# The first half's input projection reads x channel by channel: two products on raw x, token roots applied behind them, no transposes of x

## The chip, the cores and the metric

The kernel runs on one core of a Trainium2 chip. The metric is the device time of one execution in microseconds (us). The kernel before takes 2466.52 us (median of three runs, 2465.56 to 2467.81). In the profile, PE is the matrix engine (TensorE), PEld its weight loads, DVE the vector engine, ACT the scalar engine, POOL the GpSimd engine, SP the engine whose queue issues most DMAs.

## What is computed

One layer of an encoder on x, 2048 tokens of 1024 channels, in float32. Only its first step matters here: a root-mean-square norm of each token, then one wide projection.

```python
def rmsnorm(x, g):
    y = x * rsqrt(mean(x * x, axis=-1, keepdims=True) + 1e-6) * g
    return y

xn = rmsnorm(x, norm1_g[l])          # (2048, 1024)
z = xn @ w_in[l]                     # 1024 x 4608
u_pool, zq, zf, zi, zo, zg = split(z, [512, 1024, 1536, 2048, 2560])
q = silu(zq); f = lb + (1 - lb) * sigmoid(zf); v = zi
o = hgrn2(q, f, v) * silu(zo)        # gated linear recurrence
...                                  # pooling branch, gates, merge, FFN, final norm
```

The factor `rsqrt(...)` is one number for each token; it is called the token's root below.

## The kernel before

The 2048 tokens are worked through in two passes of 1024 (`b0` = 0 and 2 of the loop at the end). A pass runs `mixer` (projections, recurrence, pooling branch, output product) and `ffn`. Inside a pass, the two blocks of 512 tokens are the row halves of a Strassen-Winograd scheme: instead of eight block products each projection takes seven, P1 to P7, on sums and differences of the blocks of x (`B11`, `B21`, `B22`, `T1` to `T4`, table `FORM`) and of the weights. B11 and B21 are the low and high 512 channels of the first token block, B12 and B22 those of the second; T2 is B11 plus or minus blocks of the second token block, and so on. Each operand is split into a rounded high part and a rest (`split`: the high part by an ACT cast, the rest by a DVE subtraction), and a product is three matmuls: high by high, high by low, low by high.

The first projection of a pass, `proj_io`, computes zi and zo. It has 28 steps: seven products (order `IO_ORDER`: P1, P2, P6, P5, P7, P4, P3) times four blocks of 128 channels, each step 12 matmuls of 128x512 into four PSUM banks named `io_X`, `io_Y`, `io_Z`, `io_V` (`n_step`). In the traces its matmuls carry those names; the projections after it are called `fr_`, `gr_`, `ur_`. The weights come through `Stream`: SP loads a raw tile of 256 KB, `convert` makes the pair of parts (tile `ops`: ACT cast, DVE subtraction), at most six pairs ahead. The weights of P6 are sums of three raw tiles, made in `plan_io` (tiles `w8s` to `w11s`, line 406), on DVE.

In the first pass, the operand side works like this. `load_x_tile` loads x in rows (token on the partition). ACT squares with an accumulator give each token's sum of squares, POOL makes the root (`row_rstd`), DVE multiplies the rows by it (line 743, `x_xs`). PE transposes 128x128 pieces (line 829, `x_t`), so that channels lie on the partitions; ACT and DVE read the transposed tiles from PSUM, apply the gain and make the two parts (`scaled`, lines 868 and 869). The second token block is treated the same way a little later by `forms_b_task`. PE runs 44 more transposes of `ident` that nobody reads (`warm`): 24 ahead of the first x and five behind each of the first four row tiles. The masks of the recurrence are made on POOL by `setup_task` (lines 643 to 672), started ahead of P7 and let run when the task is stepped. The Tile scheduler decides where the instructions of these tasks stand on each engine; hand-set ties (`behind`, `stream.pins`) hold some of them.

In the second pass (`b0` = 2) the same projection already takes x channel by channel (`channel_forms`).

Of the kernel before, what the change touches and what calls it, by code (L numbers as in the profile page):

```python
# [18 lines left out]
P = 128  # L19
# [45 lines left out]
GO_AT = 3  # L65
LEAD = 5
X_AT = 8
WARM = 24, 5
GO_IO = (("P2", 1), ("P2", 0))
G_POOL = 4  # L70
CW_AT = 2
# [9 lines left out]
N_OPS = 6  # L81
LOOKAHEAD = 4
MM_PER_TICK = 6


@with_exitstack
def tile_trunk(
# [28 lines left out]
    def slot(name, cols=TB, dt=F32):  # L116
        return slots.tile([P, cols], dt, tag="s", name=name, padded_shape=[P, 528])
# [248 lines left out]
    def plan_one(key, src):  # L366
        r = stream.raw(src)
        stream.op(key, lambda nm, r=r: r.tile, [r])

    SUM_OF = {"P5": "s1", "P6": "s2", "P7": "s3", "P3": "s4"}  # L370

    def plan_io(b0):
        sevens = {}
        for p in IO_ORDER:
            for k in range(4):

                q = [w_io[k, :, c * 512 : (c + 1) * 512] for c in (0, 3, 1, 2)]
                one = {"P1": 0, "P2": 1, "P4": 3}
                if p in one:
                    plan_one("io", q[one[p]])  # L380
                    continue
                if b0:
# [16 lines left out]
                def fn(nm, k=k, p=p, raws=raws):  # L399
                    if p != "P6":  # L400
                        keep(("io", k, p), raws[0].tile, True)
                        return raws[0].tile
                    t = raws[0].tile
                    for i, r in enumerate(raws[1:]):
                        t2 = slot(f"{nm}s{i}")
                        dve.tensor_tensor(t2, t, r.tile, ALU.add)
# [195 lines left out]
    cols = const.tile([P, at], F32, tag="cols", name="cols")  # L602
    act.dma_start(cols, params)

    for j in range(1, NT):
        load_x_tile(0, j)
    for _ in range(N_RAW):
        stream.load()

    def col(o):  # L610
        return cols[:, o : o + 1]

# [2 lines left out]

    neghalf = const.tile([P, 4], F32, tag="neghalf", name="neghalf")
    pool.memset(neghalf, -0.5)

    lbt = const.tile([P, 4, 4], F32, tag="lbt", name="lbt")

# [87 lines left out]
    def warm(n, other=None):  # L708
        ps = bank("warm", P)
        for _ in range(n):  # L710
            ins = pe.transpose(ps, ident, ident)
            if other is not None:
                behind(ins, other)

    last_root = [None]

# [16 lines left out]
    def norm_rows(src, name, xs, after, lag=1):  # L733
        for j in range(NT):
# [8 lines left out]
                dve.tensor_scalar(t[hf], halves[hf], r[:, 0:1], None, ALU.mult)  # L743
                xs[j, hf] = t[hf]
            after(j)

    def load_channels(b, k):
        t = slot(f"xc{b}_{k}")
        sp.dma_start(t, x_ct[k * P : (k + 1) * P, b * TB : (b + 1) * TB])
        return t  # L750

    def root_rows(b, name):
        ss = small.tile([P, 2, 4], F32, tag="ssx", name=f"{name}ss")
# [273 lines left out]
        return forms, first, Task(channels_b_task(b + 1, gain, forms, full, go))  # L1027

    def need(forms, key, late):
        task = forms["task"][0] if key in ("B11", "B21") else late  # L1030
        while len(forms[key]) < 4:
            task.step()
        return forms[key]


# [376 lines left out]
    def proj_io(b0, forms, late, vd, zd):  # L1412
# [40 lines left out]
        for p in IO_ORDER:  # L1453
# [6 lines left out]
            for k in range(4):  # L1460
# [30 lines left out]
                        after(p, j)  # L1491
                stream.used(1)

    def mixer(b0, forms, late):
# [5 lines left out]
        proj_io(b0, forms, late, vd, zd)  # L1500
        if b0 == 0:
# [518 lines left out]
        return nxt[0] if nxt else None  # L2020


    nxt = forms_of("x", 0, o_n1, early=True, go=lambda: go_io[0])
    for _ in range(5):
        nxt[1].step()
    load_rows(1)
    while len(nxt[0]["B11"]) < 4:
        nxt[1].step()
# [5 lines left out]
    dve.tensor_tensor(lbt[:, 2], lbt[:, 0], lbt[:, 0], ALU.subtract)  # L2034
    dve.tensor_scalar(lbt[:, 3], lbt[:, 2], -1.0, 1.0, ALU.mult, ALU.add)
    for b in range(0, SEQ // TB, 2):
        forms, task, late = nxt
        if b:
            join(task)
        forms, task, late = mixer(b, forms, late)  # L2040
        join(task)
        nxt = ffn(b, forms, late)
# [51 lines left out]
```

## Time and profile before

| | us |
|---|---|
| median of 3 runs | 2466.52 |
| the profiled execution's own time | 2465.07 |
| its span in the trace | 2463.4 |
| DVE busy in it | 1921.5 |
| ACT busy in it | 1229.6 |
| POOL busy in it | 776.4 |

The span is what the trace covers; the time has 1.7 us around it. Busy times are sums of the recorded durations. A row of the timeline gives start and duration in us, engine, line, operation, output and inputs by name, shape and count; in brackets stands the idle time ahead of it and what ended it. A duration runs from the moment an instruction's semaphores are met to its end, so a wait inside the engine is part of it. Two rows that follow each other may overlap by some 0.08 us.

### The profile page before, as it was taken

What the parts mean: (1) busy time and instruction counts of PE and PEld (TensorE: products, weight loads), DVE (VectorE), ACT (ScalarE), POOL (GpSimd) and SP (SyncE); (2) the same over time, 40 slices, a digit from 0 to 9 for tenths busy, and PEclk for the clock granted to TensorE, in tenths of its full rate; (3) what the DMA queues carried; (4) which work ended last, traced back from release to release, by engine and by line L of the source; (5) the groups of instructions that cost most, each with busy time, mean ns of one, the idle gap of its engine ahead of it and who ended that gap; (6) DMA issues with size and microseconds to landing.
All of it is one profiled execution on the core that took longest, in us unless ns stands there. A gap on an engine that the chain in (4) does not pass through costs nothing.

```text
span 2463.4 us, 37815 instructions
## 1 busy us (share of the span) xinstructions
PE 2441.2 (99%) x12624; PEld 1977.9 (80%) x12624; DVE 1921.5 (78%) x3310; ACT 1229.6 (50%) x2368; POOL 776.4 (32%) x1080
## 2 busy tenths in 40 slices
PE   9999999999999999999999999999999999999998
PEld 7887777788888888888878888887888888888887
DVE  7777776897998778885596667779889987778755
ACT  6545544435555454553545455542465554445534
POOL 5343353403444333551320101122033332335310
PEclk9999999999999999999999999999999999999999
DMA  8889887777898789897554343456333444447852
GB/s 273 273 221 270 246 220 234 242 231 252 204 262 235 224 226 243 268 361 241 171 193 158 132 131 121 155 201 229 129 130 125 151 156 133 146 146 257 307 167 98
DMA packets 260226, 502.53 MB, mean 204 GB/s; under 512 B 27264, under 2 KB 47872, under 8 KB 259712
## 3 DMA queue, kind: packets, MB, share of 16 engines
q1 hardware_dynamic: 192176, 321.73, 39.8%
q0 software_dynamic: 42880, 113.27, 18.0%
q10 hardware_dynamic: 24976, 65.13, 7.6%
q8 instruction: 99, 1.62, 0.3%
q14 instruction: 95, 0.78, 0.1%
HBM read 388.35 MB, written 189.27 MB: 234 GB/s over the span
## 4 chain that ended last, share of the span: by engine, by line
PE 75%; DVE 5%; issue 1%; DMA 1%; ACT 1%; POOL 1%; SPq 0%; ACTq 0%; DVEq 0%; POOLq 0%
PE dn_P L155 16%; PE up_Z L155 15%; PE up_X L155 10%; PE up_V L155 10%; PE wo_P L155 5%; PE pb L155 3%; PE gr_X L155 2%; PE gr_V L155 2%; DVE ops L252 1%; PE io_Z L155 1%; PE fr_X L155 1%; PE io_V L155 1%; PE fr_V L155 1%; PE gr_Z L155 1%; PE gr_Y L155 1%
## 5 line engine op out<-in xcount | busy, mean ns | idle before, releaser
L251 ACT CAST ops<-raw 128x512 fp32r<-128x512 f32 x792 | 487.3, 620 | 765.5 <-PE dn_P L155 168.2
L252 DVE TENSOR_TENSOR ops<-raw,ops 128x512 fp32r<-128x512 f32 x792 | 589.6, 749 | 235.5 <-ACT ops L251 224.7
L1827 DVE SCALAR_TENSOR_TENSOR e<-h,cols,e 128x512 f32<-128x512 f32 x176 | 143.0, 817 | 30.6 <-ACT e L1825 23.0
L1825 ACT ACTIVATE e<-h,cols 128x512 f32<-128x512 f32 x176 | 142.2, 814 | 25.3 <-DVE h L1275 18.9
L1084 POOL DMA_DIRECT2D g_P<-dg_P x154 | 84.4, 549 | 172.0 <-PE dn_P L155 127.3
L1830 DVE SCALAR_TENSOR_TENSOR e<-h,cols,e 128x512 f32<-128x512 f32 x176 | 133.9, 770 | 2.5
L1396 POOL TENSOR_TENSOR gf_P<-e,e 128x512 f32<-128x512 f32 x44 | 61.0, 1389 | 148.9 <-DVE e L1836 85.9
L473 POOL TENSOR_TENSOR raw<-raw,raw 128x512 f32<-128x512 f32 x36 | 52.9, 1469 | 99.3 <-DVE ops L252 74.0
L1396 POOL TENSOR_TENSOR gf_P<-gf_P,e 128x512 f32<-128x512 f32 x44 | 58.7, 1333 | 74.0 <-DVE e L1836 71.7
L1834 ACT ACTIVATE e<-e 128x512 f32<-128x512 f32 x88 | 55.6, 632 | 36.9 <-DVE e L1830 36.7
L1820 POOL COPY h<-h 128x2 f32<-128x2 f32 x88 | 39.6, 462 | 107.3 <-DVE h L1274 99.7
L1822 POOL COPY hist<-h 128x2 f32<-128x2 f32 x88 | 36.8, 419 | 101.2 <-DVE h L1275 99.1
L1275 DVE TENSOR_TENSOR h<-up_u,up_V 128x512 f32<-128x512 f32 x88 | 60.1, 683 | 10.3 <-PE up_V L155 9.8
L1820 POOL COPY h<-hist 128x2 f32<-128x2 f32 x88 | 45.4, 521 | 54.2 <-ACT ops L251 35.6
L1371 DVE TENSOR_TENSOR x<-x,wo_P 128x512 f32<-128x512 f32 x88 | 55.9, 682 | 6.0 <-PE wo_P L155 5.8
L1536 POOL TENSOR_TENSOR q<-q,qs 128x512 f32<-128x512 f32 x16 | 22.3, 1396 | 120.0 <-ACT qs L1535 120.0
L1371 DVE TENSOR_TENSOR ac<-ac,dn_P 128x512 f32<-128x512 f32 x72 | 47.2, 682 | 12.3 <-PE dn_P L155 12.0
L1569 ACT ACTIVATE gt<-gt,cols 128x512 f32<-128x512 f32 x48 | 34.8, 725 | 43.1 <-DVE gt L1275 41.8
L1315 ACT COPY up_e<-up_X 128x512 f32<-128x512 f32 x44 | 25.8, 587 | 60.9 <-PE up_X L155 39.1
L1850 POOL DMA_DIRECT2D dg_P<-gf_P x88 | 51.2, 581 | 8.9 <-POOL gf_P L1396 7.2
L719 POOL TENSOR_SCALAR ro<-so 128x4 f32<-128x4 f32 x16 | 4.6, 285 | 146.5 <-ACT sq L1248 146.2
L1710 POOL TENSOR_TENSOR ya<-ya,gl 128x512 f32<-128x512 f32 x24 | 36.7, 1550 | 26.1 <-DVE ya L1707 17.6
(1348 smaller groups left out, 7878.4 us busy)
## 6 DMA issues: line engine op xcount, KB each, us to landing
g_P<-dg_P POOLq DMA_DIRECT2D x154, 256.0 KB, 5.6
raw<-in_w_up_t SPq DMA_DIRECT2D x132, 256.0 KB, 3.1
raw<-in_w_in_t SPq DMA_DIRECT2D x98, 256.0 KB, 3.6
dg_P<-gf_P POOLq DMA_DIRECT2D x88, 256.0 KB, 3.8
dg_P<-e SPq DMA_DIRECT2D x66, 256.0 KB, 3.3
raw<-in_w_dn SPq DMA_DIRECT2D x66, 256.0 KB, 4.2
x<-in_x SPq DMA_DIRECT2D x64, 256.0 KB, 4.8
gd<-gt ACTq DMA_DIRECT2D x64, 256.0 KB, 3.6
```

The source lines that it names most:

```text
L155: count[1] = pe.matmul(*args, **kw)
L251: self.mark = act.copy(hi, v)
L252: low = self.low = dve.tensor_tensor(lo, v, f32(hi), ALU.subtract)
L1084: eng.dma_start(t, d)
L1275: return dve.tensor_tensor(dst, t, ps, ALU.add if how == "add" else ALU.subtract)
L1371: dve.tensor_tensor(t, t, ps[j], ALU.add if sg > 0 else ALU.subtract)
L1396: pin(eng.tensor_tensor(t, x0, x1, op))
L1820: pool.tensor_copy(h[:, 0:2], hist[:, mt] if hf == 0 else hs[s, 0][:, TB : TB + 2])
L1825: in_turn(act.activation(t, h[:, 2:], AF.Identity, bias=col(o_cb + mt), scale=col(o_cw + 4 * MF + mt)))
L1827: in_turn(second(dve.scalar_tensor_tensor(t, h[:, 1 : 1 + TB], col(o_cw + 2 * MF + mt), t, ALU.mult, ALU.add)))
L1830: dve.scalar_tensor_tensor(t, h[:, 0:TB], col(o_cw + mt), t, ALU.mult, ALU.add)
L1834: in_turn(act.activation(g, g, AF.Silu))
```

## The change

The first pass's projection gets a function of its own, `first_io`; `proj_io` is left for the second pass alone. It changes these things:

- x of both token blocks is loaded transposed from the start (`x_ct`, 16 tiles of 128 channels x 512 tokens, 256 KB each, named `xc`), in an order written out in `FIRST_LOADS`, mixed with the first eight weight tiles. The row loads, the 64 transposes, the row norms and 20 of the `warm` transposes go.
- P1 and P2 take raw x times the gain (`hi_lo`, tiles `xr..h` and `xr..l`), without the root. Both add into the same four banks `io_X`; P1's share is copied out (`io_e`) before P2 adds to it. The root is applied per token when a bank is read: in `out_v(0, j)` by ACT, in `less` and `out_z(0, j)` by DVE.
- The sums of squares now run across partitions: 16 tiles of squares (`sq`, ten on ACT and six on DVE), 14 additions (`plus`, six on POOL and eight on DVE), then for each token block four matmuls of a 128x128 piece by a column of ones (`total`), a POOL power, and four matmuls that spread the roots over the partitions (`spread`), copied by ACT to `rt0` or `rt1`. These matmuls stand inside steps 3, 4, 5 and 6 of the 28.
- T2, T1, T3, T4 and B22 come from `xc`, the gains and `rt` by elementwise work on DVE and POOL from SBUF: POOL gets the products for B21 (`n21`), the subtractions for T1, T3, T4 (`n12`, `n3`, `n4`) and the additions for B22 (`n22`). B11 and B21 are split for the later projections at steps 22 to 27.
- The eight additions for the weights of P6 move from DVE to POOL (`six`, line 412 of the new kernel).
- What is done before which step is a table (`before`, `inside`), and every PE, ACT, DVE and POOL instruction of the function is tied behind the one traced before it on its engine, so their order is the written one.

```diff
-WARM = 24, 5
+WARM = 24
+FIRST_LOADS = ((0, 0), None, (0, 1), None, (0, 2), None, (0, 3), None, (0, 4), (0, 5),
+               (0, 6), (0, 7), None, (1, 0), (1, 4), None, (1, 1), (1, 5), (1, 2), (1, 6),
+               None, (1, 3), (1, 7), None)
...
+                def six(k=k, raws=raws):
+                    if k in io_sums:
+                        return
+                    while raws[-1].tile is None:
+                        stream.load()
                     t = raws[0].tile
                     for i, r in enumerate(raws[1:]):
-                        t2 = slot(f"{nm}s{i}")
-                        dve.tensor_tensor(t2, t, r.tile, ALU.add)
+                        t2 = slot(f"w6{k}s{i}")
+                        pool.tensor_tensor(t2, t, r.tile, ALU.add)
                         t = t2
                         keep(("io", k, "P6" if i else "P5"), t)
-                    return t
+                    io_sums[k] = t
...
-    load_x_tile(0, 0)
+    for at in FIRST_LOADS:
+        if at is None:
+            stream.load()
+        else:
+            xc[at] = load_channels(*at)
...
+    def first_io(vd, zd):
...
+        def hi_lo(k):
+            t, g = xc[0, k], col(o_n1 + k)
+            hi, lo = (slot(f"xr{k}{c}", TB, F32R) for c in "hl")
+            act.activation(hi, t, AF.Copy, scale=g)
+            dve.scalar_tensor_tensor(lo, t, g, f32(hi), ALU.mult, ALU.subtract)
+            raw["P1" if k < 4 else "P2"].append((hi, lo))
...
+        def square(b, k, eng=act):
+            t = sq[b, k] = slot(f"sq{b}_{k}")
+            if eng is act:
+                act.activation(t, xc[b, k], AF.Square)
+            else:
+                dve.tensor_tensor(t, xc[b, k], xc[b, k], ALU.mult)
+        def plus(b, to, k, eng=pool):
+            eng.tensor_tensor(sq[b, to], sq[b, to], sq[b, k], ALU.add)
+        def total(b):
+            ps = bank(f"ss{b}", NT)
+            for j in range(NT):
+                pe.matmul(ps[:, j : j + 1], sq[b, 0][:, j * P : (j + 1) * P], ones,
+                          start=True, stop=True)
+            m[b] = small.tile([P, 4], F32, tag="ssx", name=f"m{b}")
+            dve.tensor_scalar(m[b], ps, 1.0 / D, EPS, ALU.mult, ALU.add)
+            r[b] = roots[:, b]
+            last_root[0] = pool.tensor_tensor(r[b], m[b], neghalf, ALU.pow)
+        def spread(b):
+            ps = bank(f"rr{b}")
+            for j in range(NT):
+                pe.matmul(ps[:, j * P : (j + 1) * P], r[b][:, j : j + 1].to_broadcast([P, P]),
+                          ident, start=True, stop=True)
+            rt[b] = slot(f"rt{b}")
+            act.copy(rt[b], ps)
...
+        def n12(k):
+            norm(t1, "t1", 1, k)
+            pool.tensor_tensor(t1[k], t1[k], b11[k], ALU.subtract)
+        def n22(k):
+            b22.append(slot(f"b22{k}"))
+            pool.tensor_tensor(b22[k], t2[k], t1[k], ALU.add)
...
+        before = {
+            0: [S(hi_lo, 1), S(w), S(square, 0, 0), S(square, 0, 1), S(plus, 0, 0, 1),
+                S(hi_lo, 2), S(w), S(square, 0, 2), S(plus, 0, 0, 2), S(square, 0, 3),
+                S(plus, 0, 0, 3), S(square, 0, 4, dve), S(square, 0, 5, dve),
+                S(plus, 0, 4, 5)],
...
+            9: [S(n12, 0), S(lo, "T2", t2, 3), S(w), S(n12, 1), S(g21, 2), S(g21, 3)],
+            10: [S(n12, 2), S(n12, 3), S(f, "T1", t1, 0), S(w)],
...
+        inside = {(3, 2): [S(square, 1, 5)], (3, 3): [S(total, 0), S(square, 1, 2), S(plus, 1, 5, 2)],
+                  (4, 3): [S(spread, 0)], (5, 3): [S(total, 1), S(sums_io, 1)],
+                  (6, 2): [S(spread, 1)]}
```

Three places show the order that results. On PE, inside P1, the kernel before had transposes of x (`x_t`) between the matmuls of the third and fourth channel block:

```order
L155 MATMUL io_X_292<-ops_348,x_f3h 128x512 x2
L155 MATMUL io_X_292<-ops_348,x_f3l 128x512
L155 MATMUL io_X_293<-ops_348,x_f3h 128x512
L829 MATMUL x_t_385<-ident,x_xs_1_163 128x128
L829 MATMUL x_t_385<-ident,x_xs_1_183 128x128
L829 MATMUL x_t_385<-ident,x_xs_1_203 128x128
L829 MATMUL x_t_385<-ident,x_xs_1_223 128x128
```

In the changed kernel the same step (fourth channel block, step 3) holds the four matmuls by the column of ones, `ss`, ahead of its last bank:

```order
L158 MATMUL io_X_189<-ops_250,xr3h 128x512 x2
L158 MATMUL io_X_189<-ops_250,xr3l 128x512
L1545 MATMUL ss_326<-ones,sq_0_209 128x1 x4
L158 MATMUL io_X_190<-ops_250,xr3h 128x512 x2
L158 MATMUL io_X_190<-ops_250,xr3l 128x512
```

The transposes are gone; whatever follows on PE now stands behind `sq_0`, the finished sum of squares of the first token block.

On DVE, in the stretch of P1 and P2, the kernel before had parts read from PSUM (`x_t`), row products (`x_xs`, two short ones for each row tile) and weight parts (`ops`):

```order
L252 TENSOR_TENSOR ops_459<-raw_115,ops_459 128x512
L869 SCALAR_TENSOR_TENSOR x_f4l<-x_t_323,cols,x_f4h 128x512
L889 TENSOR_SCALAR x_b_332<-x_t_323,cols 128x512
L869 SCALAR_TENSOR_TENSOR x_f5l<-x_t_353,cols,x_f5h 128x512
L889 TENSOR_SCALAR x_b_362<-x_t_353,cols 128x512
L743 TENSOR_SCALAR x_xs_0_334<-x_0_0_242,x_0r 128x512
L743 TENSOR_SCALAR x_xs_1_335<-x_0_1_244,x_0r 128x512
```

Now it has squares, their additions and parts, and all of these read two tiles of SBUF:

```order
L1540 TENSOR_TENSOR sq_4_229<-sq_4_229,sq_6_255 128x512
L1524 SCALAR_TENSOR_TENSOR xr4l<-xc_4_94,cols,xr4h 128x512
L1540 TENSOR_TENSOR sq_4_229<-sq_4_229,sq_7_274 128x512
L1540 TENSOR_TENSOR sq_0_209<-sq_0_209,sq_4_229 128x512
L1537 TENSOR_TENSOR sq_0_278<-xc_0_104 128x512
L255 TENSOR_TENSOR ops_280<-raw_102,ops_280 128x512
L1537 TENSOR_TENSOR sq_4_297<-xc_4_106 128x512
L1524 SCALAR_TENSOR_TENSOR xr5l<-xc_5_96,cols,xr5h 128x512
```

The first and third of these rows add squares made on ACT; the fourth adds POOL's partial sum and finishes the tile that PE's `ss` reads.

On POOL the kernel before had, after the roots, the masks of the recurrence (small tiles `hist`, `uhist`, `m`):

```order
L643 MEMSET uhist 128x64
L643 MEMSET hist 128x64
L645 AFFINE_SELECT uhist<-uhist 128x64
L645 AFFINE_SELECT hist<-hist 128x64
L647 AFFINE_SELECT uhist<-uhist 128x64
L647 AFFINE_SELECT hist<-hist 128x64
L654 CAST m_912<-uhist 32x16 x4
```

In the changed kernel there stand the power, additions of squares, the weight sums of P6 (`w60s` to `w63s`), the products for B21, two DMA issues and the first T1 (`t_581`), one after the other (the rows below end ahead of the last three of these); the masks begin 32 rows behind the first row shown:

```order
L1550 TENSOR_TENSOR roots<-m_331,neghalf 128x4
L1540 TENSOR_TENSOR sq_5_319<-sq_5_319,sq_2_334 128x512
L1540 TENSOR_TENSOR sq_5_319<-sq_5_319,sq_3_346 128x512
L412 TENSOR_TENSOR w60s_362<-raw_198,raw_207 128x512
L412 TENSOR_TENSOR w60s_365<-w60s_362,raw_221 128x512
L1550 TENSOR_TENSOR roots<-m_407,neghalf 128x4
L412 TENSOR_TENSOR w61s_410<-raw_253,raw_283 128x512
L412 TENSOR_TENSOR w61s_413<-w61s_410,raw_306 128x512
L412 TENSOR_TENSOR w62s_481<-raw_355,raw_430 128x512
L412 TENSOR_TENSOR w62s_484<-w62s_481,raw_445 128x512
L412 TENSOR_TENSOR w63s_542<-raw_447,raw_449 128x512
L412 TENSOR_TENSOR w63s_545<-w63s_542,raw_499 128x512
```

Up to the first T1 POOL has 17 additions or products of 128x512 where it had none.

More of the change, by code (lines that the diff above doesn't have):

```diff
@@ L368, in plan_one @@
         stream.op(key, lambda nm, r=r: r.tile, [r])
+    io_sums, io_make = {}, {}
     SUM_OF = {"P5": "s1", "P6": "s2", "P7": "s3", "P3": "s4"}
@@ L586, in load_rows, with load_channels @@
             load_x_tile(b, j)
-    load_x_tile(0, 0)
+    def load_channels(b, k):
+        t = slot(f"xc{b}_{k}")
+        sp.dma_start(t, x_ct[k * P : (k + 1) * P, b * TB : (b + 1) * TB])
+        return t
+    xc = {}
+    for at in FIRST_LOADS:
[3 more added lines that the diff above has]
+            xc[at] = load_channels(*at)
     ident = const.tile([P, P], F32, tag="ident", name="ident")
@@ L603, in tile_trunk @@
     act.dma_start(cols, params)
[L605 to L608, printed above, removed]
     def col(o):
@@ L617, in tile_trunk @@
     pool.memset(neghalf, -0.5)
+    ones = const.tile([P, 1], F32, tag="ones", name="ones")
+    pool.memset(ones, 1.0)
+    roots = const.tile([P, 2, 4], F32, tag="roots", name="roots")
     lbt = const.tile([P, 4, 4], F32, tag="lbt", name="lbt")
@@ L706, in n_step, with warm @@
         mm(ps, b, w[:, 0], start=False, stop=last, **kw)
-    def warm(n, other=None):
+    def warm(n):
         ps = bank("warm", P)
         for _ in range(n):
-            ins = pe.transpose(ps, ident, ident)
-            if other is not None:
-                behind(ins, other)
+            pe.transpose(ps, ident, ident)
     last_root = [None]
@@ L1029, in need @@
     def need(forms, key, late):
-        task = forms["task"][0] if key in ("B11", "B21") else late
         while len(forms[key]) < 4:
-            task.step()
+            (forms["task"][0] if key in ("B11", "B21") else late).step()
         return forms[key]
@@ L1499, in mixer @@
         md, od, gd = {}, {}, {}
-        proj_io(b0, forms, late, vd, zd)
-        if b0 == 0:
+        if b0:
+            proj_io(b0, forms, late, vd, zd)
+        else:
+            forms = first_io(vd, zd)
             join(setup[0])
@@ L2020, in ffn @@
         return nxt[0] if nxt else None
[L2023 to L2028, printed above, removed]
+    warm(WARM)
     lg = cols[:, o_lb : o_lb + 4]
@@ L2036, in tile_trunk @@
     for b in range(0, SEQ // TB, 2):
-        forms, task, late = nxt
         if b:
+            forms, task, late = nxt
             join(task)
+        else:
+            forms = late = None
         forms, task, late = mixer(b, forms, late)
```

185 lines of the change are left out of this document (177 added, 8 removed).

## The prediction

> **What bounds the kernel now.** I read the page first, its busy times and its chain.
>
> ```profile
> span 2463.4 us, 37815 instructions
> PE 2441.2 (99%) x12624; PEld 1977.9 (80%) x12624; DVE 1921.5 (78%) x3310; ACT 1229.6 (50%) x2368; POOL 776.4 (32%) x1080
> PE 75%; DVE 5%; issue 1%; DMA 1%; ACT 1%; POOL 1%; SPq 0%; ACTq 0%; DVEq 0%; POOLq 0%
> ```
>
> PE is busy for all but 22.2 us. So what counts is when PE gets through the changed stretch: a shift there should reach the end. The timeline of PE gives the marks: the end of the first `warm` (1.42 + 5.01 = 6.43), the first product, the first step of P5 and the next, and the first P1 and P6 of the projection behind the changed one (`fr_`).
>
> ```profile
> 1.42 5.01 PE L711 MATMUL warm<-ident 128*128 128x128 f32 x24 [1.42 <-POOL ident L593]
> 13.82 2.13 PE L155 MATMUL io_X<-ops,x_f0h 128*128 128x512 f32 x8
> 53.31 1.32 PE L155 MATMUL io_V<-ops,x_T10h 128*128 128x512 f32 x5
> 56.08 1.08 PE L155 MATMUL io_V<-ops,x_T11h 128*128 128x512 f32 x4
> 97.76 0.39 PE L155 MATMUL fr_X<-x_f0h,ops 128*128 128x512 f32 x1
> 100.54 0.39 PE L155 MATMUL fr_Z<-x_T20h,ops 128*128 128x512 f32 x1
> L829 PE MATMUL x_t<-ident,x_xs 128*128 128x128 f32 x64 | 8.8, 276 | 2.7 <-DVE x_xs L743 2.7
> 13.82:97.76 83.94, 83.41 (x386) 68.25 (x385) 73.72 (x117) 50.01 (x95) 34.93 (x76) 1.00 0.83 257
> ```
>
> From 53.31 to 97.76 are 16 steps without a gap: 2.78 us a step, 0.231 a matmul. In the last row (busy times of PE, PEld, DVE, ACT, POOL in that stretch) PE misses 0.5 us of 83.94, and DVE is second with 73.72. DVE is thus close behind PE here, and the change gives DVE and POOL more to do.
>
> **The port of DVE and POOL.** This is where I expect the result to be decided. The timelines of both engines show it at four places:
>
> ```profile
> 89.29 1.30 POOL L473 TENSOR_TENSOR raw<-raw,raw 128x512 f32<-128x512 f32 x1 [8.57 <-DMA zd<-z]
> 89.41 1.73 DVE L686 TENSOR_TENSOR x_B223l<-x_b,x_B223h 128x512 fp32r<-128x512 f32 x1 [0.20 <-ACT x_B223h L685]
> 91.07 2.47 DVE L1274 TENSOR_TENSOR z<-io_Z,io_e 128x512 f32<-128x512 f32 x4
> 90.67 1.63 POOL L473 TENSOR_TENSOR w29s<-raw,raw 128x512 f32<-128x512 f32 x1
> 92.27 1.30 POOL L473 TENSOR_TENSOR raw<-raw,raw 128x512 f32<-128x512 f32 x1
> 741.76 1.93 DVE L1827 SCALAR_TENSOR_TENSOR e<-h,cols,e 128x512 f32<-128x512 f32 x1
> 741.82 1.31 POOL L1396 TENSOR_TENSOR gf_P<-gf_P,e 128x512 f32<-128x512 f32 x1
> 1229.80 2.95 POOL L1951 TENSOR_TENSOR fo<-fo,fg 128x512 f32<-128x512 f32 x1 [3.56 <-ACT fo L1950]
> 1230.32 0.68 DVE L252 TENSOR_TENSOR ops<-raw,ops 128x512 fp32r<-128x512 f32 x1
> 323.89 1.02 POOL L720 TENSOR_TENSOR ro<-ro,neghalf 128x4 f32<-128x4 f32 x1
> 324.06 0.69 DVE L252 TENSOR_TENSOR ops<-raw,ops 128x512 fp32r<-128x512 f32 x1 [1.20 <-DMA su2s<-in_w_up_t]
> ```
>
> A DVE row that reads two SBUF tiles takes 0.68 alone. Beside a POOL addition of 128x512 it takes 1.73, and ends 0.55 after the addition does (91.14 against 90.59): it has waited for all of it. The next DVE row reads PSUM (`io_Z`) and goes on undisturbed beside POOL at 92.27. At 741.76 a row of the three-input kind waits in the same way (1.93). At 1229.80 it is POOL that waits (2.95 for 1.30) while DVE runs several such rows back to back. So a 128x512 POOL addition and a DVE row with two SBUF inputs exclude each other. The last pair limits this: a POOL power on 128x4 leaves DVE at 0.69.
>
> **The change, part by part.** *PE.* It loses 64 transposes (8.8) and 20 of `warm`. It gains eight matmuls of one column and eight of 128x128, which no row shows in this place; the transposes of this size, 276 ns at most, bound the 16 from above (4.4), nothing from below; I take 3 us. The first product can start at 6.43, behind `warm`, since x lands early:
>
> ```profile
> 4.54 0.61 ACT L726 ACTIVATE x_xs<-x 128x512 f32<-128x512 f32 x1
> 10.92 0.62 ACT L251 CAST ops<-raw 128x512 fp32r<-128x512 f32 x1 [0.61 <-DMA raw<-in_w_io]
> 62.17 0.62 ACT L685 CAST x_T30h<-x_t 128x512 fp32r<-128x512 f32 x1 [3.71 <-DVE x_t L950]
> 62.70 0.62 ACT L251 CAST ops<-raw 128x512 fp32r<-128x512 f32 x1
> ```
>
> The first 256 KB are there by 4.54 and the ninth load by 10.92, 0.8 us each; weights and x now alternate, so a step's two tiles come every 1.6 us against PE's 2.78. Loads are no more than before and hide behind PE. ACT does one row in 0.53 us (62.17 to 62.70); its 60 rows up to the end of P6 make 32 us, so it hides too. One wait is added on PE: P2 adds into P1's banks (before, it had `io_Y` to itself), so its first matmul in a bank waits for ACT's copy of P1's share.
>
> ```profile
> 28.31 2.03 ACT L1436 COPY io_e<-io_X 128x512 f32<-128x512 f32 x4
> ```
>
> A copy is 0.5 us, and nine matmuls on the three other banks (2.1) lie between; behind the waiting matmul all of PE is queued. I cost it at nothing; with ACT late by a few rows it would be 1 us, and the delays found below hide that. If nothing else held PE, `fr_X` would start at 6.43 + 28 x 2.78 + 3 = 87.3, 10.5 earlier than now.
>
> *DVE and POOL up to the first step of P5.* I count rows in the new order, from the first rest of raw x to the weight rest of that step. On DVE 62 rows, of which 60 read two SBUF tiles: 40 of two inputs, 20 with a scalar between.
>
> ```profile
> L252 DVE TENSOR_TENSOR ops<-raw,ops 128x512 fp32r<-128x512 f32 x27 | 18.2, 685 | 3.3 <-ACT ops L251 3.3
> 14.46 0.68 DVE L252 TENSOR_TENSOR ops<-raw,ops 128x512 fp32r<-128x512 f32 x1
> 15.06 0.74 DVE L869 SCALAR_TENSOR_TENSOR x_f1l<-x_t,cols,x_f1h 128x512 fp32r<-128x512 f32 x1
> 15.72 0.68 DVE L252 TENSOR_TENSOR ops<-raw,ops 128x512 fp32r<-128x512 f32 x1
> 39.87 0.68 DVE L406 TENSOR_TENSOR w10s<-raw,raw 128x512 f32<-128x512 f32 x1
> 40.59 0.69 DVE L406 TENSOR_TENSOR w10s<-w10s,raw 128x512 f32<-128x512 f32 x1
> ```
>
> From start to start these take 0.60 and 0.66 (14.46, 15.06, 15.72), and 0.12 more where a row needs the one right ahead of it (39.87 to 40.59), which holds eight times: 40 x 0.60 + 20 x 0.66 + 8 x 0.12 = 38.2. POOL has 17 rows of 128x512 up to the first T1. Each holds the port between 1.24 (1.30 less what DVE overlaps) and 1.30: 17 x 1.27 = 21.6. Together 59.8 us on one port, from 5.3 (x at 4.54 plus an ACT row) on. It is idle a little, while POOL issues two DMAs and while a result goes round through PE (`total`, `spread`): 3 us by my count of the rows, bounds 0 and 6. The weight rest of P5's first step is then ready at 68.1, and 11 of its 12 matmuls follow (2.5): that step ends at **70.6**, where before it ended at 56.08. PE waits on the way in front of `total`, `spread` and inside P6. So of the 10.5 us that PE could gain nothing is left, and 14.5 are lost: `fr_X` at 112.3.
>
> *POOL's queue behind it.* POOL is in order, and the masks, the T3, T4 and B22 sums and the DMA issues now stand ahead of the weight sum that `fr_Z` needs (before, the POOL row at 90.67). Behind the first T1 stand 19 more additions, six DMA issues, the masks and `inv`:
>
> ```profile
> L172 POOL DMA_DIRECT2D raw<-in_w_io x8 | 7.1, 951 | 23.0 <-DVE x_T31l L686 14.0 <-DVE io_u L1442 5.5 <-DVE x_T33l L686 3.0
> L654 POOL CAST m<-hist 32x16 uint8<-32x16 f32 x12 | 4.6, 383 | 0.5
> L654 POOL CAST m<-uhist 32x16 uint8<-32x16 f32 x16 | 3.8, 235 | 0.6
> L645 POOL TENSOR_SCALAR_AFFINE_SELECT uhist<-uhist 128x64 f32<-128x64 f32 x4 | 2.5, 627 | 0.1
> L672 POOL TENSOR_SCALAR inv<-inv 128x16 f32<-128x16 f32 x4 | 2.2, 562 | 0.3
> ```
>
> Additions 19 x 1.30 = 24.7, DMA issues 6 x 0.95 = 5.7, and some 20 for masks and `inv` as recorded (the casts alone 8.4; the seven pairs of selects about 7.6), which is 11 without the waits in them. From 66 on that ends between 107 and 116, and with 0.3 us of waiting for DVE at each addition at 122. PE wants it at 112.3 + 2.8 = 115.1. So this term adds between nothing and 7 us; I take 4.5. **Sum:** +19 us, of which 14.5 from the port ahead of P5 and 4.5 from POOL's queue. Behind `fr_Z` PE again has work ready, as before, and nothing gives the loss back. The profiled execution took 2465.07 (1.45 under the median): 2465.1 + 19 = **2484 us**.
>
> The Trainium skill, SBUF — State Buffer, section "Who interferes with whom", states that DVE and GpSimd exclude each other for the whole instruction, whatever the GpSimd instruction is, if it reads SBUF. The pair at 323.89 does not show this for a small POOL row. By that rule the mask rows would hold DVE off as well; that case is the third rival.
>
> **The rivals.** *DVE and POOL get along (faster).* The exclusion costs little if POOL's additions fall into DVE's waits for ACT and DMA. Then DVE alone sets the pace: 5.3 + 38.2 + 3 = 46.5, the step ends at 49 instead of 56.08, and the time is 2465.1 - 7 = 2458. It decides once the DVE rows of P1 to P6 stay near 0.7. For it: POOL could wait at no cost while DVE is busy, as at 1229.80. Against it: POOL's rows are themselves awaited (squares, weights of P6), so both lists must be through by the same moment.
>
> *A wash.* Half of POOL's additions ahead of P5 (11 of the 21.6 us) find DVE waiting for ACT, PE or a load anyway, and POOL's queue, that much earlier, ends ahead of PE: 14.5 - 11 = +3.5, 2468.6. Of such idle time the DVE rows before show little (3.3 us in front of all its `ops` rows up to 98), which speaks against it.
>
> *All POOL rows exclude.* The masks and DMA issues then hold DVE off too, and are held off: behind 68.1 come POOL's own 50.4 (24.7 + 5.7 + 20), and of DVE's 31 two-input rows from P5 to P3 (19 us) a good half, 11, that POOL must sit out. The sum for `fr_Z` is there at 130 instead of 100.54: +29, 2494.
>
> **How the numbers follow.** Chances: the forecast 0.60, all rows exclude 0.13, a wash 0.11, get along 0.16. Its own range is 2475 to 2492 (no idle port and no queue term; both at their ends). The range of 8 in 10 leaves out the faster case and a tail of the slowest: 2461 to 2497. About 0.2% (5 us) is what a measurement of this kernel can tell from no change: faster 0.16, same 0.11, slower 0.73.
>
> **What would show it.** In the changed profile: first product near 6.4; DVE rows `sq`, `xr`, `ops`, `t` of 1.3 to 2 us instead of 0.7 wherever a POOL addition runs; PE waiting for DVE or ACT before `ss`, before `rr` and in `io_Z`; the step behind the first of P5 at about 70; `fr_X` at 110 to 115; PE waiting for the `fr_Z` weights, released from POOL. I am wrong if these DVE rows stay at 0.7, or if PE reaches `fr_X` before 98.

## The result, and the profile after

The changed kernel takes 2497.84 us (median of 4 runs, 2497.28 to 2498.91) against 2467.16 for the kernel before in the same session: ratio 1.0126, 95% interval 1.0108 to 1.0143. It is slower by 30.7 us. The prediction said 2484 and 2461 to 2497: the direction was right, the size was 14 us short, and the time lies 0.8 us above the range.

First the page of the changed kernel: its span, its busy times, and the shares of the chain that ended last.

```profile
span 2495.6 us, 37715 instructions
PE 2443.3 (98%) x12572; PEld 1975.7 (79%) x12572; DVE 1953.8 (78%) x3306; ACT 1234.4 (49%) x2360; POOL 828.4 (33%) x1101
PE 83%; DVE 5%; issue 2%; DMA 2%; POOL 1%; ACT 1%; ACTq 0%; SPq 0%; DVEq 0%; POOLq 0%
```

PE is busy for 2.1 us more than before, and the span is 32.2 longer: some 30 us are waiting. Where PE waits, up to 150 us, shows in the view of its waits (engine, what it waits for, then total, number, longest):

```profile
PE io_V L158 <- DVE ops L255: 17.0, 1, 17.0
PE ss L1545 <- DVE sq L1540: 3.8, 2, 3.3
PE io_Z L158 <- DVE xT20l L1615: 2.9, 1, 2.9
PE io_Z L158 <- ACT xT20h L1610: 2.3, 1, 2.3
PE io_X L158 <- DVE ops L255: 2.2, 2, 1.6
PE rr L1555 <- POOL roots L1550: 1.9, 1, 1.9
```

The waits before `ss`, before `rr` and in `io_Z` are the ones the prediction named. The one of 17.0 is a single event, at P5's first step. The timelines of PE, DVE and POOL there (start, duration, engine, line, output and inputs; `x4` groups four rows, whose durations run together):

```profile
63.81 0.40 PE L158 MATMUL io_V<-ops,xT10h 128*128 128x512 f32 x1
81.24 0.79 PE L158 MATMUL io_V<-ops,xT10h 128*128 128x512 f32 x1 [17.03 <-DVE ops L255]
86.09 0.73 PE L158 MATMUL io_V<-ops,xT11h 128*128 128x512 f32 x2
127.77 0.39 PE L158 MATMUL fr_X<-xB110h,ops 128*128 128x512 f32 x1
130.57 0.40 PE L158 MATMUL fr_Z<-xT20h,ops 128*128 128x512 f32 x1
64.06 16.48 DVE L709 TENSOR_TENSOR xT10l<-t,xT10h 128x512 fp32r<-128x512 f32 x1
80.47 0.72 DVE L255 TENSOR_TENSOR ops<-raw,ops 128x512 fp32r<-128x512 f32 x1
63.53 1.78 POOL L175 DMA_DIRECT2D raw<-in_w_io  x2
64.68 3.13 POOL L1578 TENSOR_TENSOR t<-t,b 128x512 f32<-128x512 f32 x2
67.13 5.57 POOL L1622 TENSOR_TENSOR t<-b,t 128x512 f32<-128x512 f32 x4
72.02 3.10 POOL L1574 TENSOR_TENSOR b<-b,rt 128x512 f32<-128x512 f32 x2
74.46 5.52 POOL L1626 TENSOR_TENSOR t<-b,t 128x512 f32<-128x512 f32 x4
79.32 0.75 POOL L666 MEMSET uhist<- 128x64 f32 x1
```

One DVE row, 0.68 of work, stands for 16.48 us. Over just that time POOL runs twelve additions back to back, 1.22 from start to start, and DVE ends 0.56 after the last of them (79.98 to 80.54). Behind that row wait the weight rest `ops` and PE; P5's second step (`xT11h`) starts at 86.09. A little earlier the same engines with the same kinds of rows had taken turns:

```profile
38.62 1.75 DVE L1563 SCALAR_TENSOR_TENSOR b<-xc,cols,rt 128x512 f32<-128x512 f32 x1
40.29 1.79 DVE L255 TENSOR_TENSOR ops<-w60s,ops 128x512 fp32r<-128x512 f32 x1
38.22 1.60 POOL L412 TENSOR_TENSOR w61s<-w61s,raw 128x512 f32<-128x512 f32 x1
39.79 1.75 POOL L412 TENSOR_TENSOR w62s<-raw,raw 128x512 f32<-128x512 f32 x1
```

Here each row waits for one row of the other engine, and no more (DVE 1.75 and 1.79, POOL 1.60 and 1.75). So the question for the experiments: why does POOL keep the port twelve times over at 64 us, and give it up after each row at 38? What differs in the rows is the pair of DMA issues at 63.53, which stand right ahead of the long run. The trace of the kernel before has the same picture, small:

```profile
709.36 0.60 POOL L1850 DMA_DIRECT2D dg_P<-gf_P  x1
709.98 1.31 POOL L1396 TENSOR_TENSOR gf_P<-e,e 128x512 f32<-128x512 f32 x1
711.23 1.30 POOL L1396 TENSOR_TENSOR gf_P<-gf_P,e 128x512 f32<-128x512 f32 x1
710.03 3.05 DVE L252 TENSOR_TENSOR ops<-raw,ops 128x512 fp32r<-128x512 f32 x1
```

A DMA issue, two additions right behind it, and a DVE row that sits out both. (A second such place is at 1921.30, where a DVE row that begins late in the first of two additions, at 1922.58, sits out the second as well and takes 2.44.)

**Theory:** a run of POOL additions that follows right behind a POOL DMA issue keeps the port shared with DVE until the run ends; without the issue the two take turns. **Rivals:** any run of ready POOL additions keeps the port; or the sum of both engines' rows on the port sets the end anyway, and the long row is only how it shows.

### The profile page after: what moved, and what is told of

The parts are those of the page before. It is cut to its first block, busy times and chain, and to the rows that moved or that the text cites. A ratio compares the mean times of both kernels' runs of the same rounds, so it can differ in the third digit from the quotient of the medians.

```text
span 2495.6 us, 37715 instructions
## 1 busy us (share of the span) xinstructions
PE 2443.3 (98%) x12572; PEld 1975.7 (79%) x12572; DVE 1953.8 (78%) x3306; ACT 1234.4 (49%) x2360; POOL 828.4 (33%) x1101
## 4 chain that ended last, share of the span: by engine, by line
PE 83%; DVE 5%; issue 2%; DMA 2%; POOL 1%; ACT 1%; ACTq 0%; SPq 0%; DVEq 0%; POOLq 0%
PE dn_P L158 16%; PE up_Z L158 14%; PE up_X L158 9%; PE up_V L158 9%; PE wo_P L158 6%; PE gr_V L158 3%; PE pb L158 3%; PE gr_X L158 3%; PE gr_Y L158 2%; PE gr_W L158 2%; DVE ops L255 1%; PE gr_Z L158 1%; PE fr_X L158 1%; PE fr_V L158 1%; PE io_Z L158 1%
```

## The experiments

All times are medians beside runs of the kernel before on the same chip in the same session (2466.5 to 2469.5). Marks are from each kernel's profile: the second matmul of P5's first step (the one that waits for the weight rest) and `fr_X`.

| kernel | time | ratio to before (95%) | P5, second matmul | `fr_X` |
|---|---|---|---|---|
| before | 2467.16 | | no wait | 97.76 |
| changed | 2497.84 | 1.0126 (1.0108 to 1.0143) | 81.24 | 127.77 |
| DMA issues early | 2491.59 | 1.0102 (1.0073 to 1.0132) | 67.18 | 116.50 |
| DMA issues late | 2491.36 | 1.0102 (1.0069 to 1.0134) | 66.30 | 118.95 |
| all on DVE | 2472.76 | 1.0019 (1.0005 to 1.0033) | 58.63 | 104.44 |
| POOL reads nothing | 2465.03 | 0.9992 (0.9981 to 1.0004) | no wait | 98.38 |

### The DMA issues moved ahead of a pause

```diff
-  9: [S(n12, 0), S(lo, "T2", t2, 3), S(w), S(n12, 1), S(g21, 2), S(g21, 3)],
-  10: [S(n12, 2), S(n12, 3), S(f, "T1", t1, 0), S(w)],
+  9: [S(lo, "T2", t2, 3), S(w), S(g21, 2), S(g21, 3)],
+  10: [S(n12, 0), S(n12, 1), S(n12, 2), S(n12, 3), S(f, "T1", t1, 0), S(w)],
```

> The changed kernel with one move: the first two subtractions of T1 go behind the weights of their step, so that POOL's queue has all four accumulating DMA issues ahead of them, where POOL has to wait for a DVE row before it goes on; in the changed kernel two of these issues stand right ahead of twelve additions that are ready. Theory (a run of POOL additions that follows right behind a POOL DMA issue keeps the port until the run ends): no DVE row over 3 us; the two engines take turns, DVE rows of 1.6 to 1.8; PE's wait of 17.0 for the weight rest of P5's first step becomes 2 to 5; fr_X at 115 to 119 in place of 127.8; time 2484 to 2490. Rival one (any run of ready POOL additions keeps the port): a DVE row of 12 us or more again, 2495 to 2500. Rival two (the port sum alone sets the end, the long row is only how it shows): no long row, but PE waits as much in other places, fr_X at 125 or later, 2494 to 2498.

Measured: 2491.59, and up to 130 us no DVE row over 1.81 us. POOL's and DVE's timelines of this kernel:

```profile
50.04 3.80 POOL L175 DMA_DIRECT2D raw<-in_w_io  x4
59.85 6.73 POOL L1578 TENSOR_TENSOR t<-t,b 128x512 f32<-128x512 f32 x4 [6.01 <-DVE t L1563]
66.54 6.38 POOL L1622 TENSOR_TENSOR t<-b,t 128x512 f32<-128x512 f32 x4
63.70 1.75 DVE L709 TENSOR_TENSOR xT10l<-t,xT10h 128x512 fp32r<-128x512 f32 x1
65.38 1.75 DVE L255 TENSOR_TENSOR ops<-raw,ops 128x512 fp32r<-128x512 f32 x1
```

Between the DMA issues and the additions POOL now waits 6.01 us for DVE. The same additions take turns with DVE: four in 6.4 to 6.7 us, and the row that stood 16.48 takes 1.75. The first four each follow a DVE product that they read; the four behind (66.54) wait for nothing and take turns all the same. PE's wait of 17.0 has become one of 3.93, and `fr_X` comes 11.3 us sooner. The first rival is out, and so is the second. Nor is it enough that any POOL row stands right ahead: in the kernel before two additions follow a POOL copy without a pause, at 671.77, and the DVE row beside them (672.29) takes its turn with 1.78. The time is 1.6 over the theory's range: of the 11.3 us only 6 arrive at the end, since behind `fr_X` PE waits for 6.2 us once, at `pl`, for an ACT row `k` that itself waits for a DMA. Why that transfer is late in this kernel was not followed.

### The DMA issues moved into the run

```diff
-  15: [S(f, "T3", t3, 1), S(w), S(n4, 0), S(n4, 1)],
+  15: [S(f, "T3", t3, 1), S(w), S(adds), S(n4, 0), S(n4, 1)],
```

`adds` issues the two later accumulating DMAs, which are held back until then.

> The changed kernel with the two later accumulating DMA issues of POOL moved from ahead of the third T1 subtraction to ahead of the four T4 subtractions; the additions keep their order. Theory (a run behind a DMA issue keeps the port): the eight additions ahead of the DMA issues take turns with DVE (DVE rows of 1.6 to 1.8), and one DVE row stands 5 to 7.5 us (the issues and four additions of 1.22) right behind them; PE waits some 2 to 4 us at P5's first step and 3 to 6 us at that row; time 2485 to 2492. Rival one (any run of ready additions keeps the port): a DVE row of 9 us or more already ahead of the DMA issues; 2494 to 2499. Rival two (port sum alone): no row over 3 us, 2494 to 2498.

Measured: 2491.36, from two runs that lie 6 us apart (2488.33 and 2494.40); the profile is of the first. The timelines show both behaviours in one run of additions:

```profile
65.66 6.41 POOL L1626 TENSOR_TENSOR t<-b,t 128x512 f32<-128x512 f32 x4
72.01 2.97 POOL L1578 TENSOR_TENSOR b<-b,rt 128x512 f32<-128x512 f32 x2
74.92 1.79 POOL L179 DMA_DIRECT2D raw<-in_w_io  x2
76.08 5.63 POOL L1630 TENSOR_TENSOR t<-b,t 128x512 f32<-128x512 f32 x4
73.78 1.75 DVE L259 TENSOR_TENSOR ops<-raw,ops 128x512 fp32r<-128x512 f32 x1
75.45 6.82 DVE L713 TENSOR_TENSOR xT13l<-t,xT13h 128x512 fp32r<-128x512 f32 x1
```

Ahead of the DMA issues four additions take 6.41, in turns; behind them four take 5.63, back to back, and one DVE row stands for 6.82. The long row has moved with the DMA issues, and it has shrunk with the run behind them: (16.48 - 6.82) / 8 = 1.21 us for each addition fewer. The time, both DVE figures and PE's wait at P5's first step (3.33) are as the theory expected; PE's wait at the held row is smaller, 1.90 against 3 to 6, as it had already waited 2.84 one step earlier.

### A memset between issue and run

```diff
-  10: [S(n12, 2), S(n12, 3), ...
+  10: [S(apart_by_memset), S(n12, 2), S(n12, 3), ...
```

> The changed kernel with one added POOL row: a memset of 128x4 that nobody reads, between the two accumulating DMA issues and the third T1 subtraction. Question: does the hold need an addition right behind the DMA issue, or is it enough that the issue and the additions stand in one run without a pause? In the changed kernel DVE got the port when POOL came to a memset. If a row that reads no SBUF hands the port on: no DVE row over 3 us, as with the DMA issues moved (2491), so 2487 to 2493, fr_X at 115 to 120. If the state set by the DMA issue lasts over it: the DVE row stands 14 to 17 us again, 2494 to 2499.

Measured: 2495.79, and the hold is there as before:

```profile
62.51 1.77 POOL L175 DMA_DIRECT2D raw<-in_w_io  x2
63.63 0.76 POOL L1578 MEMSET gap<- 128x4 f32 x1
63.70 3.13 POOL L1582 TENSOR_TENSOR t<-t,b 128x512 f32<-128x512 f32 x2
63.03 16.51 DVE L710 TENSOR_TENSOR xT10l<-t,xT10h 128x512 fp32r<-128x512 f32 x1
```

A small row that reads no SBUF does not hand the port on. In the rows one sees a sign of the held state: each POOL row begins before the POOL row ahead of it has ended (63.70 inside the memset; two additions of 1.9 within 3.13), and this starts inside the second DMA issue. Where the engines take turns, each POOL row starts as the POOL row ahead of it ends. (The two additions at 709.98 lack the sign: the second needs the result of the first.) The hold reaches back into the issue: the DVE row here begins at 63.03, 0.6 us ahead of the memset, while POOL has only the two issues in hand, and yet it does not get through. Beside a DMA issue with no addition behind it such a row takes 0.69 (at 69.99 in the kernel before). In the changed kernel the DVE row gets through as the last addition ends (79.98), while POOL is in the memset of `uhist`. What in the chip makes this state was not tried.

### All of POOL's rows on DVE

The edit replaces `pool.tensor_tensor` by `dve.tensor_tensor` in `plus`, `six`, `n21`, `n12`, `n22`, `n3` and `n4`. In the trace of the changed kernel these are 34 rows (6, 8 and five times 4); the expectations count 36.

> The changed kernel with all 36 two-input rows of POOL in this stage (the square sums, the weight sums of P6, the forms B21, T1, T3, T4, B22) on DVE, at the same places of the text. POOL keeps its DMA issues, powers and masks. By the sum of the prediction a DVE row holds the port for 0.60 to 0.66 where a POOL row holds it for 1.27: 20 rows ahead of P5's first step make 12.6 on DVE, 38.2 + 12.6 + 8.3 = 59.1, the step ends at 61.6 (56.1 before the change), 5.5 over the kernel before; time 2467 to 2474, fr_X at 100 to 106. Rival (DVE as a whole is too full in this stage, so what leaves the port comes back as DVE's own time): 2480 or more. Rival (masks and powers of POOL hold DVE off too): DVE rows over 1.2 us beside masks, 2475 or more.

Measured: 2472.76, 25 us under the changed kernel. The second matmul of P5's first step stands at 58.63; with the 2.54 that the rest of the step took before the change it would end at 61.2 (61.6 expected). In the trace the next step starts at 62.72, as PE runs slower behind its waits (granted clock 0.87 from 45 to 60 us, 0.90 from 60 to 75). POOL's masks and powers remain beside DVE, and their rows show what is not excluded:

```profile
48.98 0.87 POOL L668 TENSOR_SCALAR_AFFINE_SELECT uhist<-uhist 128x64 f32<-128x64 f32 x1
51.16 2.08 POOL L677 CAST m<-uhist 32x16 uint8<-32x16 f32 x4
49.25 1.33 DVE L1574 TENSOR_TENSOR b<-b,rt 128x512 f32<-128x512 f32 x2
51.28 0.69 DVE L1578 TENSOR_TENSOR t<-t,b 128x512 f32<-128x512 f32 x1
22.05 2.56 POOL L1550 TENSOR_TENSOR roots<-m,neghalf 128x4 f32<-128x4 f32 x1 [17.38 <-DVE m L1548]
```

Masks cost DVE nothing: beside selects and casts one of its rows takes 0.69 and two take 1.33. The other way round it is different: the power, 1.02 at 323.89 in the trace before, takes 2.56 while DVE runs row behind row, and PE waits 2.5 us for it.

### POOL's rows that read nothing

Each of these 34 rows becomes `pool.memset` of its output; the sums of squares, the weights of P6 and the forms B21, T1, T3, T4 and B22 are left out.

> The changed kernel with each of POOL's 36 two-input rows in this stage replaced by a memset of its output: the sums of squares, the P6 weights and the forms B21, T1, T3, T4, B22 are left out, everything else stands in the same order. POOL reads no SBUF in these rows. Theory (the loss is the port between DVE and POOL): DVE rows at 0.6 to 0.75 throughout, PE waits under 8 us up to fr_X, fr_X at 88 to 93, time 2454 to 2460, some 40 us under the changed kernel. Rival (DVE's own load, ACT, loads or the waits through PE and POOL for the roots set the pace): 2475 or more, with DVE rows at 0.7 but PE waiting as before.

Measured: 2465.03, between the two expectations: the loss against the kernel before is gone, but of the 10.5 us that PE could have gained nothing is left. (A memset is also shorter than an addition, 0.53 us against 1.3, so this run alone does not part the port from POOL's own time.) `fr_X` stands at 98.38, not at 87.3. PE's waits in this kernel up to 130 us:

```profile
PE io_V L158 <- ACT ops L254: 2.8, 1, 2.8
PE rr L1558 <- POOL roots L1553: 1.7, 1, 1.7
PE io_Z L158 <- DVE xT22l L1618: 1.4, 1, 1.4
```

These and one of 0.2 are 6.1 us of the 11.1 that are missing. The granted clock, 0.89 to 0.94 from 30 to 75 us, accounts for some 3.5 more (an estimate, 45 us by the missing share); what such clock costs behind a wait the next pair of runs measures.

### The clock behind a wait

```diff
+                if n == 12:
+                    for _ in range(76):
+                        pe.transpose(bk["V"][3][:, :P], ident, ident)
```

> The changed kernel with 76 transposes of the identity ahead of P5's first step, into a bank that the step's start flag overwrites; they run while PE waits for the weight rest (63.6 to 81.2) and take some 16 us at 0.21 each. Question: what does the lower granted clock behind the wait cost? In the changed kernel the stretch from the second matmul of P5's first step to fr_X took 46.3 us, in the kernel before 44.2. If the clock falls because PE stands: with PE busy until shortly before, that stretch is 44.2 to 44.8, granted clock 0.9 or more from 75 to 90, time 1.5 to 2.2 less than the changed kernel's, 2495 to 2496.5. If the clock has another cause: no change of the stretch, 2497 to 2499.

Measured: 2498.60. The transposes took 0.11 each, not the 0.21 I had from the first warm-up, PE still stood for 8.8 us, and nothing changed: a run that decides nothing. Again with `range(155)`:

> As the run with 76 transposes ahead of P5's first step, with 155. There the transposes took 0.11 each, not the 0.21 that was assumed from the first warm-up, so they ended at 72.5 and PE stood for 8.8 us behind them; the stretch from the second matmul of P5's first step to fr_X stayed at 46.6. 155 x 0.11 = 17.0, up to about 81, with a wait of 1 us or less behind them. If the clock falls because PE stands: the stretch is 44.2 to 44.8, about 2 us less, and granted clock is near 1.0 from 75 to 90; time 2495 to 2497.5. If it has another cause: 46 or more, 2497 to 2499.5.

Measured: 2493.88 (ratio 1.0106, 1.0089 to 1.0123), 1.1 under the expected range and 4 us under the changed kernel, of which 1.4 come from an earlier end of P6, which the edit does not touch. PE's timeline of this kernel, and below it the busy times and granted clock (the third figure from the end) of the changed kernel and of this one from the second matmul on:

```profile
62.30 17.08 PE L1737 MATMUL io_V<-ident 128*128 128x128 f32 x155
79.86 0.50 PE L158 MATMUL io_V<-ops,xT10h 128*128 128x512 f32 x1 [0.24 <-DVE ops L255]
124.05 0.39 PE L158 MATMUL fr_X<-xB110h,ops 128*128 128x512 f32 x1
81.20:127.77 46.57, 46.53 (x191) 37.73 (x192) 33.87 (x52) 19.90 (x34) 30.80 (x68) 0.95 0.66 201
79.86:124.00 44.14, 44.14 (x191) 35.98 (x192) 33.41 (x52) 20.11 (x34) 29.29 (x67) 1.00 0.67 200
```

With PE busy during the hold the same 191 recorded matmuls take 44.1 us at a granted clock of 1.00, against 46.5 at 0.95. So PE's standing costs 2.3 us more behind the wait. Nearly all of it falls into the rest of P5's first step: in the changed kernel its nine matmuls from 82.25 to 86.09 take 0.43 us each, where 0.231 was the pace before. The Trainium skill, TensorE: Matmul & The Clock Gate, section "What's actually happening", says that PE falls to half its clock after a window of about 3.4 us without work and needs about as long to come back. By that the wait of 8.8 us in the first of these two runs was still too long, and the trace agrees: its stretch, 81.86 to 128.73, stayed at 46.9.

### Three tries to go below the kernel before

From the all-DVE version, six squares moved from DVE to ACT:

> The version with all of POOL's 36 rows on DVE, and the six squares that DVE makes on ACT as well (the sums of squares stay as they are). DVE loses 6 rows, 3.6 us, ahead of P5; ACT gains 6 x 0.63. Theory (DVE's rows, back to back at 0.60 to 0.66, set the pace): second matmul of P5's first step at 55 to 57 where the all-DVE version had 58.6 and the kernel before the change ended that step at 56.1; fr_X at 100 to 102; time 2467 to 2471, that is a tie with the kernel before or a little over. Rival (PE's waits for the powers on POOL and its lower clock behind them set the pace by now): fr_X at 103 to 105, 2471 to 2474.

Measured: 2472.62 (1.0019, 1.0011 to 1.0028), no gain, second matmul at 59.0. ACT was busy for 14.5 of the 15 us from 15 to 30, and PE waited 4.4 us for the last sum of squares. I had cost ACT's rows at nothing.

The 14 additions of squares moved to PE as well:

```diff
+                for k in range(8):
+                    pe.matmul(ps[:, j : j + 1], sq[b, k][:, j * P : (j + 1) * P], ones,
+                              start=not k, stop=k == 7)
```

> The version with all of POOL's 36 rows on DVE, and with DVE relieved: the squares are summed by PE (32 matmuls of one column for each half instead of 4, into one bank; the 14 additions of squares go) and the six squares on DVE go to ACT. Up to P5's first step DVE loses 20 rows, 20 x 0.62 = 12.4, against the all-DVE version, where that step's second matmul stood at 58.6; PE gains 56 matmuls of one column at 0.131 (8 took 1.05): 7.3. Theory (DVE's rows set the pace, 0.60 to 0.66 each): second matmul at 48 to 51, PE waits under 8 us up to fr_X, fr_X at 94 to 99, time 2459 to 2467. Rival (the loss of clock behind waits, and waits that go round through roots and ACT, take what DVE gives up): fr_X over 100, 2468 to 2474.

Measured: 2489.48 (1.0093, 1.0076 to 1.0110). PE's waits up to 130 us fall from 9.5 us in the all-DVE version to 7.0 (without the one at the start), but its timeline shows the price:

```profile
17.29 10.66 PE L1546 MATMUL ss<-ones,sq 128*128 128x1 f32 x64
35.74 8.83 PE L1546 MATMUL ss<-ones,sq 128*128 128x1 f32 x64
```

An fp32 matmul of one column is two rows in the trace: 32 make 64 rows and 9 to 11 us. I had read a group of 8 rows as eight matmuls where it was four. With squares in fp32r, two equal columns, and the six squares back on DVE, each is one row:

> The version with all of POOL's 36 rows on DVE, with the 14 additions of squares (8.4 us of DVE) given to PE as in the run with 64 rows a half, but on squares rounded to fp32r and with two equal columns: 32 matmuls a half in one row each, where the fp32 ones took two rows each and 10.7 and 8.8 us. The squares stay where they are. Theory (DVE's rows set the pace, and that run lost only by PE's 17 us): at 0.13 to 0.16 a row 4.2 to 5.1 a half on PE; second matmul of P5's first step at 50 to 54 (all-DVE version 58.6), fr_X at 95 to 100, time 2461 to 2468: at or just under the kernel before. Rival (PE's rows in ss stand in DVE's way as before, or ACT's squares come late): fr_X over 102, 2470 or more.

Measured: 2475.74 (1.0029, 1.0018 to 1.0040). The sums now take PE 3.63 and 4.75 us, as expected, and DVE is relieved (7.8 us busy from 15 to 30). Yet the second matmul stands at 59.65, for DVE is late behind the roots of the second half: PE comes to spreading them at 35.2 (32.98 in the all-DVE version), and what needs them (the forms T2 and T1 and their rests) follows on DVE from there, which is busy for 14.8 of the 15 us from 45 to 60. Work taken from DVE ahead of that point no longer counts. None of the three beats the kernel before.

## Why the prediction was wrong in size, step by step

The difference of the two profiled spans, 32.2 us, against the forecast's terms. The first row takes P5's first step at the clock of before, so that it ends 2.54 behind its second matmul, at 83.8; that it ended at 86.09 is the second row.

| term | forecast | measured |
|---|---|---|
| port, up to the end of P5's first step | 14.5 | 14.5 + 13.2 |
| clock behind the wait | none | 2.3 |
| POOL's queue ahead of `fr_Z` | 4.5 | 0 |
| behind `fr_X` | 0 | 2.2 |

**PE: right, with one thing missing.** The first product stands at 5.97 (6.43 said), and PE's waits before `ss`, before `rr` and inside P6 are there. No row waits for ACT's copy of P1's share, which was costed at nothing. The small matmuls (`ss` 1.05 and 1.87, `rr` 1.16 and 1.05) took 5.1 us (the 1.87 in a stretch with a granted clock of 0.77), not the 3 assumed, and over the bound of 4.4; each fp32 matmul of them is two rows. But the bound of 87.3 for PE alone took full clock and no wait: with POOL's reads gone it was 98.38. So the rival "get along" at 2458 was out of reach even without the port; its mechanism, tried, gave 2465.0.

**The port: right as a mechanism, and the sum holds.** DVE rows of 1.6 to 1.8 beside POOL's additions are what was said, and where nothing holds DVE off, the second matmul stands at 67.18 and 66.30 against 68.1 from the sum. The changed kernel says so itself: the first T1 was through at 60.6, and DVE came to the two rows of P5's first step at 64.06, so that by their own 0.68 and 0.72 they could have been done by 65.5. That 67.18 and 66.30 come so near 68.1 is partly luck. In the version with the DMA issues early, 20 additions and not 17 ran ahead of that mark, and the port stood idle for 1.6 us and not 3; the forecast's own prices with these counts give 5.3 + 38.2 + 20 x 1.27 + 1.6 = 70.5, so the prices were about 5% high. The all-DVE version says the same from the other side: with DVE's 0.60 to 0.66 for each of 20 rows in place of POOL's 1.27, its step would end at 61.2 at the clock of before, where the sum gives 61.6.

**The failed step** is the list of rows that entered that sum: "POOL has 17 rows of 128x512 up to the first T1." It let the two DVE rows of P5's first step go ahead of the additions behind, taking it that POOL gives way after each row. The runs showed in its place that POOL keeps the port for the whole run behind a DMA issue: twelve more additions came first, 12 x 1.22 = 14.6 us, and that step's end at the clock of before (83.8) lies 13.2 behind the 70.6 of the forecast. A DMA issue entered the sum only as idle time of the port. Of the signs named, the step behind the first of P5 came at 86.09 instead of about 70, and `fr_X` at 127.77 instead of 110 to 115. The row in the trace before that shows this (710.03, 3.05 us beside two additions) stands against it; the prediction quotes only places with one addition.

**The clock** had no term. PE stood for 17 us, and the matmuls behind the wait cost 2.3 us more up to `fr_X` (46.5 from the second matmul, 44.2 before the change); filling the wait takes this away.

**POOL's queue** was costed at 4.5 and is 0 in the changed kernel: `fr_Z` follows `fr_X` by 2.80, as before by 2.78. The additions that held DVE off were, for POOL, done without waiting, and PE was later still. Where the hold is gone, PE waits 0.4 to 1.0 us for `fr_Z`'s weights.

**Behind `fr_X`** the kernel before needs 2365.6 us from `fr_X` to the end, the changed one 2367.8; small waits before `pl` (4.1 against 2.2) are most of it. That "nothing gives the loss back" behind `fr_Z` was right.

**The rivals.** "All POOL rows exclude" gave 2494, nearest to the result, for another reason than the true one: masks cost DVE nothing, and what DMA issues cost lay in the additions right behind them. "A wash" needed half of POOL's additions to find DVE waiting; DVE was busy for 13.7 to 14.9 of every 15 us from 15 to 60 us in the version with the DMA issues early, and its rows were waiting for POOL instead. The Trainium skill, SBUF — State Buffer, section "Who interferes with whom", states that whoever comes first has the shared pair for the whole instruction. For additions of 128x512 the trace agrees (DVE rows of 1.75 beside one addition); for selects and casts of 128x64 and less it does not show it (0.69 beside them); and behind a DMA issue the pair was kept over twelve instructions, 16.48 us.

## What to carry to other kernels

A sum over a port that two engines share is only as good as the order in which they get it. List the waiting engine's rows, then look on the other engine for the longest run of ready rows behind a DMA issue, and take it that a row of the first may have to sit out all of it; a pause between issue and run, made by a wait that is there anyway, was worth 11 us at `fr_X` here and 6 at the end. Before moving two-input work to POOL compare the time each engine holds the port for it (1.27 against 0.60 to 0.66): here DVE was the cheaper place for all 34 rows.

## What was not expected of the hardware

- The hold itself: 16.48 us (twelve additions), 6.82 (four), 3.05 (two), each right behind a POOL DMA issue; 1.6 to 1.8 in the runs without one. A memset of 128x4 in between does not end it. It is not certain at every issue: at 2257.93 of the kernel before a DVE row that began inside one went through in 0.68, and the single addition behind the issue waited (1.45).
- A power on 128x4 on POOL takes 2.56 us instead of 1.02 when DVE runs two-input rows without a gap, though it costs DVE nothing itself.
- PE's transposes of 128x128 run at 0.11 us each with PE warm, against 0.21 (5.01 / 24) in the first warm-up.
